# A hybrid attention layer on one core: the head gates as Silu in place, the multiplications one at a time, and the probabilities split ahead of normalising

## The chip, the cores and the metric

The kernel runs on one core of one Trainium2 chip. The metric is the device time of one execution in microseconds (us). Before the change three runs gave 320.87, 321.19 and 321.32 us, a median of 321.19.

## What is computed

One decoder layer on x of 512 tokens by 1024 columns, all in float32. After an RMSNorm a single projection gives eight pieces; attention runs over two groups of eight heads of 64 columns; each group's output is multiplied by the silu of a projected gate; then come an output projection, a residual, a gated second projection and a last norm.

```python
proj = rms_norm(x, norm_g) @ w_in            # a_q a_k a_v a_g b_q b_k b_v b_g
a_out = swa_attention(a_q, a_k, a_v, sinks, bias)    # window of 128, 2 key/value heads
b_out = moba_attention(b_q, b_k, b_v, bias)          # here all past blocks plus the own one
mixed = concat([a_out * silu(a_g), b_out * silu(b_g)])
x = x + mixed @ w_out
gate = sigmoid(rms_norm(x, ple_g) @ w_ple_gate)
return rms_norm(x + (p @ w_ple_proj) * gate, final_norm)
```

## The kernel before

Every float32 operand of TensorE is split into a high part (ScalarE copies it to the format fp32r) and a low part (VectorE subtracts the copy), and each product is three matmuls: high by high, high by low, low by high. `split_T` (lines 141 to 144) does this for activations and probabilities, `Weights.split` (lines 103 to 119) for a quarter of a weight chunk. With `engines="AP"` every second low quarter is subtracted on GpSimd instead of VectorE (line 117); only the two chunks `w_bg` of the second gate are made so (line 163).

There are three phases. The first prepares the norm, the transposed activations `acts` and the small projection. The second, which the change touches, runs the remaining projections as a stream of 192 pieces and lays the attention between them. A piece is three matmuls of 512 columns, or six of 256. `block` (line 424) strings pieces together and runs the evacuation of one accumulator behind the first piece of the next block. Accumulators of the projections share two PSUM slots (tag `acc`), so a block can begin only when the block before the last has been evacuated. The order of blocks is gates and queries of the window heads (`w_qg`), then `w_bv[0]`, `w_bkq[0]`, `w_bkq[1]`, `w_bv[1]`, `w_bkq[2]`, `w_bkq[3]` and the two `w_bg`. Weights are loaded and split by `prefetch` during the sixteen pieces before they are needed.

`swa_step` (line 714) does one of 16 steps of the window heads: scores, bias and maximum (VectorE, line 554), exponential (ScalarE, 557), division, transposition, split, two selects on GpSimd (582), and the product with the values. `moba_step` (line 758) does the same for the second group, 32 steps of one head and one query block, and six to drain. In a step, scores for head h are started, a share of the stream runs, the row sums are divided out (`norm`; for the widest block on ScalarE, line 619, else on VectorE, 621), the transposed probabilities of head h-1 are split into `pt` (`moba_trans`, `split_T`), more of the stream runs, and the product of an earlier group is made by `moba_av` (line 636) from its `pt`.

The gates are evacuated raw into tiles G (`raw_g`, line 524): seven by ScalarE, the eighth by VectorE (529). `silu_gate` (532) then takes a scratch tile of the tag `aux` (two buffers, shared with the evacuations of the attention outputs), computes the sigmoid on ScalarE (534), multiplies it by G on VectorE (535), and multiplies the head outputs O by that on GpSimd (536). It is called for gates 0 to 3 behind the window steps (line 749), for 4 and 5 after the drain step m = 33, for 6 and 7 at the end, where O is split into `acts` (line 799). The tiles G are four slots, so gate 4 takes the place of gate 0.

The order of TensorE and of the transfers queued on SP is the order in which the program is written (`MANUAL`, line 34). From `early.close()` (706) to the last phase's second half (922) the order of ScalarE, VectorE and GpSimd is chosen when the program is built, by the order of the text and by which operations are ready; each engine then works through its queue in that order, and the first operation that has to wait holds up all behind it.

The third phase (from 802) has the output projection (`w_late[0]`, from line 876, four accumulators of which two are the `acc` slots), the second projection and the final norm. Its sigmoids (line 899) come late.

Of the kernel before, what the change touches and what calls it, by code (L numbers as in the profile page):

```python
# [10 lines left out]
F32 = mybir.dt.float32  # L11
BF16 = mybir.dt.bfloat16
F32R = mybir.dt.float32r
AF = mybir.ActivationFunctionType
ALU = mybir.AluOpType

P = 128
SEQ = 512
# [16 lines left out]
C_AQ, C_AK, C_AG, C_BQ, C_BK, C_BV, C_BG = 0, 512, 768, 1280, 1792, 2304, 2816  # L35
# [3 lines left out]
def hybrid_layer_kernel(  # L39
# [16 lines left out]
    nc = tc.nc  # L56
# [22 lines left out]
    def bank(shape, name, tag):  # L79
        return psum.tile(shape, F32, name=name, tag=tag)  # L80
# [75 lines left out]
    def chunk(name, cols, **kw):  # L156
        return Weights(name, [wi[:, :, c:c + n] for c, n in cols], **kw)
# [2 lines left out]
    w_qg = [chunk(f"aqg{c}", [(C_AQ + c * P, P), (C_AG + c * P, P)]) for c in range(4)]  # L160
    w_bv = [chunk(f"bv{n}", [(C_BV + n * 256, 256)]) for n in range(2)]
    w_bkq = [chunk(f"bkq{n}", [(C_BK + n * P, P), (C_BQ + n * P, P)]) for n in range(4)]
    w_bg = [chunk(f"bg{n}", [(C_BG + n * 256, 256)], engines="AP") for n in range(2)]

    def wide(src, n, name, pool=None):
        ns = slice(n * 512, (n + 1) * 512)
# [219 lines left out]
    with ExitStack() as ph2:  # L386
        def pool(name, bufs):
            return ph2.enter_context(tc.tile_pool(name=name, bufs=bufs, reuse_waits="tile"))
# [8 lines left out]
        xa = pool("xa", 2)  # L397

        O = [op.tile([P, SEQ], F32, name=f"O_{c}") for c in range(8)]
        G = {}  # L400
# [3 lines left out]
        def toep(head, swa):  # L404

            if swa:
                b = bp.tile([P, 2, 256], F32, name="b_a", tag="b")
                src = bass.AP(tensor=d_tab.tensor, offset=d_tab.offset + head * JT + JB,
                              ap=[[1, P], [JT, 2], [1, 256]])
            else:  # L410
                b = bp.tile([P, 512], F32, name="b_b", tag="b")
                src = bass.AP(tensor=d_tab.tensor, offset=d_tab.offset + (HA + head) * JT,
                              ap=[[1, P], [1, 512]])
            nc.sync.dma_start(b, src)
            return b
# [16 lines left out]
        def run(n):  # L432
            while stream and (n > 0 or stream[0][0] == 0):
                c, f = stream.popleft()
                n -= c
                f()
# [87 lines left out]
        def raw_g(c, acc):  # L524
            g = op.tile([P, SEQ], F32, name=f"G_{c}", tag=f"G_{c % 4}")
            if c < 7:
                nc.scalar.activation(g, acc, AF.Copy)
            else:
                nc.vector.tensor_copy(g, acc)  # L529
            G[c] = g  # L530

        def silu_gate(c):
            sg = xa.tile([P, SEQ], F32, name="sg", tag="aux")
            nc.scalar.activation(sg, G[c], AF.Sigmoid)
            nc.vector.tensor_mul(sg, sg, G[c])  # L535
            nc.gpsimd.tensor_mul(O[c], O[c], sg)  # L536


        def swa_scores(c, i, q, kt, bias):
            lo_k = 0 if i else P  # L540
            w = 256 - lo_k
            k0 = (i - 1) * P + lo_k
            S = bank([P, 2, 256], "S", "S")
            st = sp.tile([P, 2, 260], F32, name="st", tag="st")
            nm = small.tile([P, 2], F32, name="nm")
            sm = small.tile([P, 2], F32, name="sm")
            ri = small.tile([P, 2], F32, name="ri")
            nc.gpsimd.tensor_copy(st[:, :, 256], nsink[:, 2 * c:2 * c + 2])
            for s in range(2):
                for j in range(2):  # L550
                    nc.tensor.matmul(S[:, s, lo_k:], q[s][:, i, :], kt[:, j, k0:k0 + w],
                                     start=j == 0, stop=j == 1)
            for s in range(2):
                nc.vector.tensor_tensor_reduce(st[:, s, lo_k:256], S[:, s, lo_k:], bias[:, s, lo_k:], -1.0,  # L554
                                               nsink[:, 2 * c + s:2 * c + s + 1], ALU.add, ALU.min,
                                               nm[:, s:s + 1])
                nc.scalar.activation(st[:, s, lo_k:257], st[:, s, lo_k:257], AF.Exp,  # L557
                                     bias=nm[:, s:s + 1], scale=-1.0, accum_out=sm[:, s:s + 1])

            def norm():  # L560
                pv = st[:, :, P:2 * P]
                if i:
                    nc.gpsimd.tensor_add(pv, pv, st[:, :, 0:P])
                nc.vector.reciprocal(ri, sm)
                for s in range(2):
                    nc.vector.tensor_scalar_mul(pv[:, s], pv[:, s], ri[:, s:s + 1])
            return st, norm
# [35 lines left out]
        def moba_scores(h, i, q, kt, bias):  # L603
            w = (i + 1) * P
            S = bank([P, 512], "Sb", "S")
            st = sp.tile([P, 520], F32, name="stb", tag="st")
            nm = small.tile([P, 1], F32, name="nmb")
            sm = small.tile([P, 1], F32, name="smb")
            ri = small.tile([P, 1], F32, name="rib")
            for j in range(2):  # L610
                nc.tensor.matmul(S[:, :w], q[:, i, :], kt[:, j, :w], start=j == 0, stop=j == 1)  # L611
            nc.vector.tensor_tensor_reduce(st[:, :w], S[:, :w], bias[:, 512 - w:], -1.0, 1.0e38,  # L612
                                           ALU.add, ALU.min, nm)
            nc.scalar.activation(st[:, :w], st[:, :w], AF.Exp, bias=nm, scale=-1.0, accum_out=sm)  # L614

            def norm():
                nc.vector.reciprocal(ri, sm)
                if i == 3:
                    nc.scalar.activation(st[:, :w], st[:, :w], AF.Copy, scale=ri)
                else:  # L620
                    nc.vector.tensor_scalar_mul(st[:, :w], st[:, :w], ri)
            return st, norm
# [3 lines left out]
        def moba_trans(g, sts):  # L626
            tp = bank([P, 512], "tpb", "tp")
            o = 0
            for j in GRP[g]:
                for i in range(j, NT):  # L630
                    nc.tensor.transpose(tp[:, o:o + P], sts[i][:, tok(j)], rev)  # L631
                    o += P
            pt = pp.tile([P, 2, 512], F32R, name="pt", tag="pt")
            return lambda: split_T(pt[:, 0, :o], pt[:, 1, :o], tp[:, :o]), pt

        def moba_av(h, g, pt, oacc):
            o = 0
            for j in GRP[g]:
                w = SEQ - j * P
                for l in range(2):  # L640
                    nc.tensor.matmul(oacc[:, j * P:], Vb[:, j, h].rearrange("p a d -> p (a d)"),  # L641
                                     pt[:, l, o:o + w], start=j == 0 and l == 0, stop=j == 3 and l == 1)
                o += w
# [20 lines left out]
        for c in range(4):  # L664
            w = w_qg[c]
            proj_T(w, 0, lambda acc, c=c: make_q(qa[c], acc))
            proj_T(w, P, lambda acc, c=c: raw_g(c, acc))
            ahead(w)
# [78 lines left out]
        swa_step(16)  # L747
        swa_step(16)
        for c in range(4):
            silu_gate(c)  # L750
        run(12)


# [4 lines left out]
        def moba_step(m):  # L758
            h, i = divmod(m, 4)
            norm = None  # L760
            if h < HB:
                if i == 0 and h + 2 < HB:
                    bb[h + 2] = toep(h + 2, False)
                st, norm = moba_scores(h, i, qb[h // 2][h % 2], kb[h // 2][h % 2], bb[h])
                sts[h, i] = st
            pace(per * 0.4)
            if norm:
                norm()
            new = None
            if h > 0 and i > 0 and h - 1 < HB:  # L770
                sp_, pt = moba_trans(i - 1, [sts[h - 1, k] for k in range(NT)])
                sp_()
                new = (h - 1, i - 1, pt)
            pace(per * 0.4)
            if ptq:
                h2, g2, pt2 = ptq.popleft()
                if g2 == 0:
                    ob[h2] = bank([P, 512], "oaccb", "o")
                moba_av(h2, g2, pt2, ob[h2])
                if g2 == 2:  # L780
                    moba_evac(h2, ob[h2])
            if new:
                ptq.append(new)
            pace(per * 0.2)

        for m in range(32):
            moba_step(m)
        per = 2.0
        for m in range(32, 38):
            moba_step(m)  # L790
            if m == 33:
                for c in (4, 5):
                    silu_gate(c)
        run_all()
# [7 lines left out]
    with ExitStack() as ph3:  # L802
# [82 lines left out]
        for t in range(NT):  # L885
            acc = bank([P, 512], "acc4", tags.popleft())
# [36 lines left out]
        for n in range(2):  # L923
            for t in range(NT):
                last = n == 1 and t == NT - 1
                parts = [slice(0, 512)] if not last else [slice(0, 256), slice(256, 512)]
                for cols in parts:
                    w = cols.stop - cols.start
                    acc = bank([P, 512], "acc5", tags.popleft())
# [61 lines left out]
```

## Time and profile before

| | before |
|---|---|
| three runs | 320.87, 321.32, 321.19 us |
| profiled execution | 321.41 us, span 319.7 us, outside the span 1.7 us |
| busy, share of the span | TensorE (PE) 96%, VectorE (DVE) 71%, ScalarE (ACT) 58%, GpSimd (POOL) 21% |
| granted TensorE clock | 0.995 of full speed |
| window heads | about 44 to 125 us |
| second group of heads | about 134 to 221 us |
| output projection onward | from 219.6 us |

All stretches are in microseconds from the start of the span. TensorE's busy time counts a matmul until its modelled end, so matmuls overlap in it and a short wait can hide inside a busy stretch. In a timeline row the first number is the start, the second the duration; a bracket at the end says how long the engine had stood idle before it and whose end released it.

### The profile page before, as it was taken

The numbers are of one execution on the slowest core, as the hardware profiler recorded it, in microseconds if no ns is written. First come the engines' busy times: TensorE is split into PE (matmuls) and PEld (weight loads), VectorE is DVE, ScalarE is ACT, GpSimd is POOL, SyncE is SP. The second block draws the span as 40 slices with busy tenths as digits, with TensorE's granted clock in tenths as the row PEclk, the third lists the DMA queues.
The fourth block names the chain that finished last, engine by engine and source line by source line (L and its number), as shares of the span: only waits on it lengthen the run. The fifth ranks groups of instructions, "written<-read, shape, count | busy, mean of one in ns | idle before, by whom it ended". The sixth has DMA issues, their size and how long they took to land.

```text
span 319.7 us, 4741 instructions
## 1 busy us (share of the span) xinstructions
PE 307.7 (96%) x1651; PEld 259.8 (81%) x1651; DVE 226.3 (71%) x517; ACT 185.6 (58%) x418; POOL 66.6 (21%) x118
## 2 busy tenths in 40 slices
PE   8999999999999999899999999999999999999990
PEld 6788788888889888699888878877888888888890
DVE  2885867886787858878778787859658656672544
ACT  3766565756574638778678776787158323541341
POOL 1420102436343252600003130012300110000011
PEclk9999999999999999999999999999999999999998
DMA  7964597050406083751445303004956700000113
GB/s 237 388 166 114 152 230 232 6 133 1 131 3 199 1 196 87 178 163 37 131 98 143 90 3 131 0 0 111 381 184 248 262 2 0 2 0 0 68 67 131
DMA packets 33208, 37.61 MB, mean 118 GB/s; under 512 B 1416, under 2 KB 24976, under 8 KB 33184
## 3 DMA queue, kind: packets, MB, share of 16 engines
q1 hardware_dynamic: 32240, 34.47, 34.7%
q0 software_dynamic: 800, 2.62, 4.1%
q8 instruction: 13, 0.21, 0.3%
q10 hardware_dynamic: 144, 0.21, 0.2%
q14 instruction: 11, 0.09, 0.1%
HBM read 32.52 MB, written 2.16 MB: 108 GB/s over the span
## 4 chain that ended last, share of the span: by engine, by line
PE 73%; DVE 12%; issue 6%; ACT 4%; POOL 3%; POOLq 0%; DVEq 0%; ACTq 0%
PE acc L451 8%; PE acc L452 8%; PE acc L453 8%; PE acc L137 7%; PE acc L139 7%; PE acc L138 7%; PE acc_ple L282 4%; PE acc_akv L301 4%; PE Sb L611 3%; PE accv L137 2%; PE oaccb L641 2%; PE accv L139 2%; PE accv L138 2%; PE tpb L631 2%; DVE q L499 2%
## 5 line engine op out<-in xcount | busy, mean ns | idle before, releaser
L557 ACT ACTIVATE st<-st,nm 128x257 f32<-128x257 f32 (+1 forms) x32 | 15.2, 478 | 22.0 <-DVE nm L554 19.9
L137 PE MATMUL acc<-hi_wg,h 128*128 128x512 f32 (+1 forms) x72 | 26.7, 370 | 0.0
L139 PE MATMUL acc<-hi_wg,h 128*128 128x512 f32 (+1 forms) x72 | 26.4, 367 | 0.0
L451 PE MATMUL acc<-acts,hi_bkq 128*128 128x512 f32 x64 | 26.4, 412 | 0.0
L138 PE MATMUL acc<-lo_wg,h 128*128 128x512 f32 (+1 forms) x72 | 26.3, 365 | 0.0
L451 PE MATMUL acc<-acts,hi_aqg 128*128 128x512 f32 x64 | 26.2, 410 | 0.0
L137 PE MATMUL acc<-hi_wo,acts 128*128 128x512 f32 x64 | 25.4, 397 | 0.5 <-DVE G L529 0.5
L453 PE MATMUL acc<-acts,lo_aqg 128*128 128x512 f32 x64 | 25.2, 393 | 0.0
L453 PE MATMUL acc<-acts,lo_bkq 128*128 128x512 f32 x64 | 25.1, 392 | 0.0
L138 PE MATMUL acc<-lo_wo,acts 128*128 128x512 f32 x64 | 25.1, 392 | 0.0
L139 PE MATMUL acc<-hi_wo,acts 128*128 128x512 f32 x64 | 25.1, 392 | 0.0
L452 PE MATMUL acc<-acts,hi_bkq 128*128 128x512 f32 x64 | 25.1, 392 | 0.0
L452 PE MATMUL acc<-acts,hi_aqg 128*128 128x512 f32 x64 | 25.1, 392 | 0.0
L614 ACT ACTIVATE stb<-stb,nmb 128x128 f32<-128x128 f32 (+3 forms) x32 | 17.9, 558 | 9.0 <-DVE nmb L612 8.7
L582 POOL TENSOR_SCALAR_AFFINE_SELECT pta<-pta 128x512 fp32r<-128x512 f32 x24 | 17.3, 722 | 14.3 <-DVE pta L144 13.2
L137 PE MATMUL accv<-hi_bv,acts 128*128 128x256 f32 x64 | 18.7, 293 | 1.5 <-DVE kt L144 1.5
L536 POOL TENSOR_TENSOR O<-O,sg 128x512 f32<-128x512 f32 x8 | 11.4, 1430 | 39.4 <-DVE sg L535 39.3
L139 PE MATMUL accv<-hi_bv,acts 128*128 128x256 f32 x64 | 18.1, 282 | 0.0
L138 PE MATMUL accv<-lo_bv,acts 128*128 128x256 f32 x64 | 18.0, 281 | 0.0
L839 ACT ACTIVATE sq<-x 128x512 f32<-128x512 f32 x15 | 9.5, 630 | 13.9 <-DVE x L901 11.6
L612 DVE CUSTOM_DVE_ANT_0 stb<-Sb,b_b 128x128 f32<-128x128 f32 (+3 forms) x32 | 15.5, 485 | 2.4 <-PE Sb L611 2.3
L508 POOL DMA_DIRECT2D kt<-kt x10 | 5.6, 564 | 50.7 <-DVE kt L144 48.3
(165 smaller groups left out, 873.2 us busy)
## 6 DMA issues: line engine op xcount, KB each, us to landing
raw_aqg<-in_w_in_dram SPq DMA_DIRECT2D x8, 512.0 KB, 5.7
raw_bkq<-in_w_in_dram SPq DMA_DIRECT2D x8, 512.0 KB, 5.1
raw_wo<-in_w_out_dram SPq DMA_DIRECT2D x4, 1024.0 KB, 6.5
raw_wg<-in_w_ple_gate_dram SPq DMA_DIRECT2D x4, 1024.0 KB, 5.9
kt<-kt POOLq DMA_DIRECT2D x10, 256.0 KB, 4.5
x_t<-in_x_dram SPq DMA_DIRECT2D x4, 512.0 KB, 7.3
raw_bv<-in_w_in_dram SPq DMA_DIRECT2D x2, 1024.0 KB, 5.4
b_b<-d_tab SPq DMA_DIRECT2D x8, 256.0 KB, 5.8
```

Source lines behind the costliest of these rows:

```text
L137: nc.tensor.matmul(acc, sh, mh, start=first, stop=False)
L138: nc.tensor.matmul(acc, sh, ml, start=False, stop=False)
L139: nc.tensor.matmul(acc, sl, mh, start=False, stop=last)
L282: nc.tensor.matmul(pacc[t, n], (pTl if j == 1 else pTh)[:, k, tok(t)], (wpl if j == 2 else wph)[:, n, k], start=k == 0 and j == 0, stop=k ...
L301: nc.tensor.matmul(akv[m], w_[:, k, cs], acts[:, k, a_, :], start=k == 0 and w_ is w_akv.hi and a_ == 0, stop=k == KC - 1 and w_ is w_akv.lo)
L451: nc.tensor.matmul(acc, w.hi[:, k, cs], acts[:, k, 0, :], start=k == 0, stop=False)
L452: nc.tensor.matmul(acc, w.hi[:, k, cs], acts[:, k, 1, :], start=False, stop=False)
L453: nc.tensor.matmul(acc, w.lo[:, k, cs], acts[:, k, 0, :], start=False, stop=k == KC - 1)
L557: nc.scalar.activation(st[:, s, lo_k:257], st[:, s, lo_k:257], AF.Exp, bias=nm[:, s:s + 1], scale=-1.0, accum_out=sm[:, s:s + 1])
L582: nc.gpsimd.affine_select(out=pt[:, :, b, :].rearrange("p j (s q) -> p j s q", s=2), in_=pt[:, :, 1, :].rearrange("p j (s q) -> p j s q", ...
L612: nc.vector.tensor_tensor_reduce(st[:, :w], S[:, :w], bias[:, 512 - w:], -1.0, 1.0e38, ALU.add, ALU.min, nm)
L614: nc.scalar.activation(st[:, :w], st[:, :w], AF.Exp, bias=nm, scale=-1.0, accum_out=sm)
```

## The change

There are five edits. The low halves of `w_bg` are all made on VectorE. The eighth gate leaves PSUM as Silu on ScalarE, and not as a copy on VectorE. The other seven are turned into their silu in place by one ScalarE operation each (`silu`), which replaces the sigmoid, its scratch tile and the product on VectorE; each is issued behind the last exponential traced by then (`issue_after` puts it later in the same queue and adds no wait). The product with O is called apart, on GpSimd for gates 0 to 5 (0 to 3 after the steps 1, 4, 7 and 10 of the second group), on VectorE for 6 and 7. In `moba_step` the division `norm` is traced behind the transposition and split.

```diff
-    w_bg = [chunk(f"bg{n}", [(C_BG + n * 256, 256)], engines="AP") for n in range(2)]
+    w_bg = [chunk(f"bg{n}", [(C_BG + n * 256, 256)]) for n in range(2)]
...
             if c < 7:
                 nc.scalar.activation(g, acc, AF.Copy)
             else:
-                nc.vector.tensor_copy(g, acc)
+                with tc.issue_after(last_exp[0].ins):
+                    nc.scalar.activation(g, acc, AF.Silu)
             G[c] = g
 
         def silu_gate(c):
-            sg = xa.tile([P, SEQ], F32, name="sg", tag="aux")
-            nc.scalar.activation(sg, G[c], AF.Sigmoid)
-            nc.vector.tensor_mul(sg, sg, G[c])
-            nc.gpsimd.tensor_mul(O[c], O[c], sg)
+            (nc.vector if c >= 6 else nc.gpsimd).tensor_mul(O[c], O[c], G[c])
+
+        def silu(c):
+
+            with tc.issue_after(last_exp[0].ins):
+                nc.scalar.activation(G[c], G[c], AF.Silu)
+
+        last_exp = [None]
...
-                nc.scalar.activation(st[:, s, lo_k:257], st[:, s, lo_k:257], AF.Exp,
+                last_exp[0] = nc.scalar.activation(st[:, s, lo_k:257], st[:, s, lo_k:257], AF.Exp,
...
-            nc.scalar.activation(st[:, :w], st[:, :w], AF.Exp, bias=nm, scale=-1.0, accum_out=sm)
+            last_exp[0] = nc.scalar.activation(st[:, :w], st[:, :w], AF.Exp, bias=nm, scale=-1.0, accum_out=sm)
...
         for c in range(4):
-            silu_gate(c)
+            silu(c)
         run(12)
...
             pace(per * 0.4)
-            if norm:
-                norm()
             new = None
             if h > 0 and i > 0 and h - 1 < HB:
                 sp_, pt = moba_trans(i - 1, [sts[h - 1, k] for k in range(NT)])
                 sp_()
                 new = (h - 1, i - 1, pt)
+            if norm:
+                norm()
             pace(per * 0.4)
...
         for m in range(32):
             moba_step(m)
+            if m in (1, 4, 7, 10):
+                silu_gate((m - 1) // 3)
         per = 2.0
         for m in range(32, 38):
             moba_step(m)
             if m == 33:
+                for c in range(4, 7):
+                    silu(c)
                 for c in (4, 5):
                     silu_gate(c)
```

## Rows read from the trace of the kernel before

**Rows 1.** Windows: length, busy us (count) of PE, PEld, DVE, ACT, POOL; clock, DMA share, GB/s

```profile
128.00:141.00 13.00, 11.48 (x80) 10.39 (x80) 11.79 (x25) 8.99 (x18) 4.70 (x5) 1.00 0.59 151
141.00:162.00 21.00, 21.00 (x133) 18.85 (x133) 15.78 (x50) 15.35 (x38) 1.02 (x2) 1.00 0.42 121
162.00:192.00 30.00, 29.45 (x158) 24.61 (x158) 24.72 (x68) 23.27 (x54) 6.46 (x6) 1.00 0.32 73
...
224.00:312.00 88.00, 88.00 (x424) 73.42 (x423) 52.96 (x80) 35.03 (x75) 9.13 (x24) 1.00 0.31 110
```

**Rows 2.** Waits of the whole run: waiter, releaser, us in total, times, longest

```profile
PE oaccb L641 <- DVE pt L144: 0.6, 2, 0.4
...
PEld oaccb L641 <- DVE pt L144: 2.3, 4, 0.8
...
ACT sg L899 <- PE acc L139: 9.2, 6, 2.6
```

**Rows 3.** Timeline from the last window step to the second group's first scores

```profile
123.45 1.28 ACT L534 ACT_TABLE_LOAD   x1
...
127.89 0.63 ACT L534 ACTIVATE sg<-G 128x512 f32<-128x512 f32 x1 [1.37 <-POOL O L536]
...
128.56 3.02 DVE L535 TENSOR_TENSOR sg<-sg,G 128x512 f32<-128x512 f32 x2 [1.26 <-ACT sg L534]
...
129.80 0.59 ACT L143 ACTIVATE kt<-acc 64x512 fp32r<-64x512 f32 x1
...
131.61 0.69 DVE L144 TENSOR_TENSOR kt<-acc,kt 64x512 fp32r<-64x512 f32 x1
...
132.45 0.36 PE L137 MATMUL accv<-hi_bv,acts 128*128 128x256 f32 x1 [1.52 <-DVE kt L144]
```

**Rows 4.** Timeline of the next evacuation and the block that needs its slot

```profile
135.17 0.69 DVE L499 SCALAR_TENSOR_TENSOR q<-acc,q 64x512 fp32r<-64x512 f32 x1
...
136.01 0.36 PE L137 MATMUL accv<-hi_bv,acts 128*128 128x256 f32 x1
```

**Rows 5.** Groups by line: operation, count, busy us in total, mean ns, idle before

```profile
L118 DVE TENSOR_TENSOR lo_wo<-raw_wo,hi_wo 128x512 fp32r<-128x512 f32 x16 | 10.4, 685 | 6.2 <-ACT hi_wo L116 6.1
...
L118 DVE TENSOR_TENSOR lo_bg<-raw_bg,hi_bg 128x512 fp32r<-128x512 f32 x4 | 3.7, 922 | 0.4 <-ACT hi_bg L116 0.4
...
L118 POOL TENSOR_TENSOR lo_bg<-raw_bg,hi_bg 128x512 fp32r<-128x512 f32 x4 | 5.3, 1334 | 16.1 <-ACT hi_bg L116 16.1
...
L536 POOL TENSOR_TENSOR O<-O,sg 128x512 f32<-128x512 f32 x8 | 11.4, 1430 | 39.4 <-DVE sg L535 39.3
```

**Rows 6.** Timeline of GpSimd and VectorE ahead of a late split

```profile
185.17 1.30 POOL L118 TENSOR_TENSOR lo_bg<-raw_bg,hi_bg 128x512 fp32r<-128x512 f32 x1 [6.11 <-ACT hi_bg L116]
...
185.52 1.50 DVE L118 TENSOR_TENSOR lo_bg<-raw_bg,hi_bg 128x512 fp32r<-128x512 f32 x1
...
187.85 0.42 DVE L621 TENSOR_SCALAR stb<-stb,rib 128x384 f32<-128x384 f32 x1
188.30 0.56 DVE L144 TENSOR_TENSOR pt<-tpb,pt 128x384 fp32r<-128x384 f32 x1
```

**Rows 7.** Waits from 212 to 225 us

```profile
PEld oaccb L641 <- DVE pt L144: 1.1, 2, 0.5
```

**Rows 8.** Timeline from the last normalisation to the output projection

```profile
209.03 0.72 ACT L619 ACTIVATE stb<-stb,rib 128x512 f32<-128x512 f32 x1 [0.32 <-DVE rib L617]
...
210.79 0.60 PE L631 MATMUL tpb<-rev,stb 128*128 128x128 f32 x4
...
210.86 1.28 ACT L534 ACT_TABLE_LOAD   x1
...
214.45 0.97 DVE L535 TENSOR_TENSOR sg<-sg,G 128x512 f32<-128x512 f32 x1 [0.31 <-ACT sg L534]
...
221.57 0.69 DVE L529 COPY G<-acc 128x512 f32<-128x512 f32 x1
...
222.32 0.50 PE L137 MATMUL acc<-hi_wo,acts 128*128 128x512 f32 x1 [0.47 <-DVE G L529]
```

## The prediction

> **What bounds the kernel now.** I read the windows first, for the share of each engine in each stretch. TensorE's own work is the bound almost everywhere: from 224 us on it is busy for 88.00 of 88 us, and from 141 to 162 us for all 21.00 [rows 1]. No saving on another engine is worth anything there. What can be won is the time in which TensorE stands still, so I then listed its waits, and looked up each in the timeline. In the part that the change touches there are three.
>
> The largest, 1.52 us, is at 132.45: the first matmul of the values' projection wants an accumulator slot, and that slot is still being evacuated (kt, VectorE, 131.61) [rows 3]. Two queues made this late. On ScalarE the third sigmoid stands 1.37 us waiting for GpSimd to free its scratch tile, and the second half of the key's evacuation is queued behind the sigmoids and starts at 129.80. On VectorE two gate products take 3.02 us, 1.51 each, and kt follows them at once.
>
> The second is the product with the values, which waits for the split probabilities pt. TensorE's matmuls show 0.6 us idle in two places, its weight loads 2.3 us in four [rows 2]; two of the four, 1.1 us, fall between 212 and 225 us [rows 7], so 1.2 us fall before. The third, 0.47 us, is at 222.32, where the output projection wants the slot of the eighth gate, which VectorE copies only at 221.57 [rows 8].
>
> **The gates behind the window heads.** The change takes away four scratch tiles, four VectorE products and ScalarE's wait for GpSimd. ScalarE's work stays: four Silus instead of four sigmoids, taken at the sigmoid's 0.63 us, and the load of a table before them, 1.28 us [rows 3]. The key's second half could then start no later than 127.89, where the waiting sigmoid stood. VectorE's part would end near 128.5 + 0.69 = 129.2, and TensorE wants the slot at 132.45 - 1.52 = 130.93. So the whole 1.52 us goes.
>
> What is late next is the evacuation of the query block: it ends at 135.17 + 0.69 = 135.86, and the block that needs its slot starts at 136.01 [rows 4], so there was no slack. If TensorE comes 1.52 us earlier, the evacuation must too. It can give back between nothing (the 3.02 us of products and the late kt are gone from ahead of it) and all 1.52. I take 0.3, nearer to nothing, since its queue gains about twice what it must.
>
> **The low quarters.** Four subtractions of 1.334 us leave GpSimd and become four of 0.685 us on VectorE: 2.74 us more. The four that VectorE had already took 922 ns instead of 685 beside GpSimd [rows 5], so 4 x 0.237 = 0.95 us comes back, 1.8 us net, between 162 and 192 us where VectorE is busy for 24.72 of 30 us [rows 1]. The price on the path lies between nothing and 1.8. I take nothing: from 141 to 162 us VectorE makes all the quarters of another chunk, and TensorE has no gap there [rows 1].
>
> **Splitting ahead of dividing.** In rows 6 the late pt at 188.30 stands behind a quarter that GpSimd stretched to 1.50 us (0.82 too long) and behind a division of 0.42 us. Both go from ahead of it, another quarter comes. The division is needed a step later at the earliest, by the transpositions of the next head. Of the 1.2 us before 212 I count half, 0.6.
>
> Between 212 and 225 us VectorE loses the products of gates 4 and 5, one of 0.97 us at 214.45 [rows 8], from ahead of pt; all 1.1 us should go. Together 1.7, between the 0.6 of the matmuls' idle time and the 2.3 of the weight loads.
>
> **The eighth gate.** ScalarE evacuates it as Silu, some 0.6 us after its block. The slot is wanted at 222.32 - 0.47 = 221.85, two us after the block's end. So 0.47 us goes; it stays if ScalarE's queue has weight copies ahead of it.
>
> **The silus behind the last exponential.** This is new and costs something. Behind that exponential ScalarE idles 0.32 us until the reciprocal for its division at 209.03 is there [rows 8]. Gate 4 is ready long before, so its Silu can be queued into that gap, with its table load: free at 208.71, plus 1.28, plus 0.63, the division starts at 210.62 and ends at 211.34. The transpositions that need it run at 210.79, so TensorE would lose 0.55. With two silus in the gap it is 1.18, with none nothing. I take 0.5. Before, the load stood at 210.86, behind the division.
>
> **The products on GpSimd.** Four of 1.430 us [rows 5] move from about 126 to 133 us into the steps of the second group, unless the queue takes them as soon as they are ready. GpSimd has 1.02 us of work there [rows 1]. VectorE pays: a two-input operation beside GpSimd went from 0.685 to 1.50 us [rows 5, 6], so up to 4 x 0.82 = 3.3 us, with 21 - 15.78 = 5.2 us idle in that stretch. Their cost is between nothing and 3.3; I take nothing, with VectorE's idle time as cover. Transfers of kt issued from GpSimd's queue may start up to 1.43 us later; their keys are used several steps on.
>
> In rows 6 GpSimd runs from 185.17 to 186.47, and VectorE's subtraction from 185.52 to 187.02. The Trainium skill, page "SBUF — State Buffer", section "Who interferes with whom", says that a VectorE instruction with two SBUF inputs and a GpSimd instruction that reads SBUF exclude each other: the later one waits for the whole of the earlier. By that rule the subtraction would end at 186.47 + 0.685 = 187.16; the trace has 187.02, so it agrees within 0.14 us. By the rule the four products could block VectorE for 5.7 us instead of 3.3, which speaks against the change (an estimate).
>
> **Edits at no cost.** The two products of gates 6 and 7 on VectorE stand where TensorE has 88 us of work without a gap [rows 1]; the gates are needed only after six eighths of the first output block. A further table load before the sigmoids of line 899 (no row shows whether one is needed) costs between nothing and 1.28; ScalarE waits 9.2 us for TensorE in front of them [rows 2], so nothing. No transfer of the SP queue is moved.
>
> **Sum.** 1.52 + 1.7 + 0.47 - 0.3 - 0.5 = 2.89 us. The profiled execution took 321.41, 0.22 over the median of 321.19. Against the median: 318.3 us.
>
> **Rivals.** (A) ScalarE takes the silus as blocks. Behind the window heads 1.28 + 4 x 0.63 = 3.8 us would stand ahead of an evacuation and could rebuild the 1.52 us; at the end two silus cost 1.18 instead of 0.5. That gives 318.3 + 1.5 + 0.7 = 320.5. For it: nothing but readiness keeps them apart. Against: each goes into the queue only where ScalarE has nothing older.
>
> (B) The wait only moves. TensorE, early by 1.52, waits for the query's evacuation for all of it, 1.2 more than I took, and the two late splits before 212 stay: 318.3 + 1.2 + 0.6 = 320.1. For it: rows 4 show no slack. Against: the 3.02 us that leave VectorE.
>
> (C) Slower: VectorE becomes the bound between 141 and 192 us. It gains 1.8 us of quarters and 3.3 us of collisions, and if each step waits for its pt, all 5.1 us reach TensorE, and the 0.6 does not come: 318.3 + 5.1 + 0.6 = 324.0. It decides from the point where pt ends after TensorE wants it in most steps. For it: 24.72 of 30 us, and two late splits there. Against: they are two among some sixteen groups, and 141 to 162 us runs without a wait.
>
> (D) The queues don't do what the text says: the eighth Silu behind the weight copies, the 0.47 stays: 318.8.
>
> **The numbers.** The forecast has 0.60, A 0.13, B 0.12, C 0.09, D 0.06. The range begins at 321.19 - (1.52 + 2.3 + 0.47) = 316.9, with every wait gone and nothing given back, and reaches to 320.4, over B and D and up to A; C is left out. A difference of 0.2%, 0.64 us, is about the least that a measurement of this kernel tells from none, so faster is below 320.55: the forecast, D, and most of A and B, 0.80. Same takes the rest of A and B, 0.09. Slower is C and a little for what I don't see, 0.11.
>
> **What would show it.** Right: no gap of TensorE near 131 us, the key's evacuation done before 130; pt ahead of the division on VectorE; no wait on G at the output projection; from then on the same work, some 3 us earlier. The 0.5 shows as a table load between the last exponential and the division of line 619. Wrong: waits of line 641 on pt in many steps (C), a gap at the second values' block (B), four Silus in a row ahead of a key's evacuation (A). If the gap at 131 is gone and the time is still the same, the sum's mistake lies in what is late next.

## The result and the profile after

Four runs of each kernel on one chip: before 321.16 us (320.87 to 321.32), after 317.84 us (317.46 to 318.12). The ratio on record is 0.9891 with an interval of 0.9879 to 0.9904 (the two medians alone give 0.9897): faster by 3.32 us, about 1%. The forecast was 318.3, within 316.9 to 320.4. The profiled execution of after took 317.72 us, 316.0 of them the span and 1.7 outside it, as before.

The page's first part (TensorE's share is up by one point, VectorE's and GpSimd's are down), and behind it the first and the third window of [rows 1]:

```profile
PE 306.3 (97%) x1651; PEld 259.7 (82%) x1651; DVE 218.7 (69%) x514; ACT 186.5 (59%) x419; POOL 58.1 (18%) x112
```

```profile
128.00:141.00 13.00, 12.58 (x93) 11.89 (x92) 8.41 (x26) 8.78 (x20) 0.51 (x1) 1.00 0.73 194
...
162.00:192.00 30.00, 30.00 (x163) 25.48 (x162) 26.59 (x73) 23.75 (x55) 1.12 (x2) 1.00 0.30 77
```

From 128 to 141 us TensorE is busy for 12.58 us instead of 11.48. From 162 to 192 us TensorE has no gap any more. VectorE has 26.59 us of work there instead of 24.72, but the two windows do not hold the same work, since after is about 2 us ahead. The groups by line compare like with like: the low quarters `lo_bg` take VectorE 5.4 us instead of 3.7 [rows 5], near the 1.8 more that the prediction worked out.

The waits of the whole run on these places, answering [rows 2]:

```profile
PE accv L137 <- DVE q L499: 0.4, 1, 0.4
...
PE oaccb L646 <- DVE pt L144: 0.2, 1, 0.2
...
PEld oaccb L646 <- DVE pt L144: 0.5, 1, 0.5
```

The waits on `pt` fell from 0.6 to 0.2 (matmuls) and from 2.3 to 0.5 (weight loads). A wait on `q` is new.

**Where the time came from.** Both traces hold the same 1651 matmuls in the same order, so the start of the n-th matmul can be set against its start before. The shift between them changes in a few places only (0.1 us and more; the next matmul's share of 0.1 is counted in):

| start of the matmul, before and after | what it had waited for | change, us |
|---|---|---|
| 132.45, 130.44 first values' block | evacuation of the key, `kt` | -1.68 |
| 136.01, 134.34 second values' block | evacuation of the query, `q` | +0.41 |
| 171.11, 169.14 product with the values | `pt` | -0.31 |
| 188.91, 186.43 product with the values | `pt` | -0.67 |
| 211.12, 208.67 last transpositions | division of line 624 | +0.14 |
| 214.19, 211.48 product with the values | `pt` | -0.42 |
| 222.32, 218.79 output projection | eighth gate | -0.75 |

That is -3.28 us. Ahead of them the shift changes by some 0.3 us in the first 20 us, at the first transfers and the warm-up, which the change does not touch and which differ from one execution to another (by up to 1 us in the runs below). So I count from matmul 121 (line 267, at about 23 us) to the end: 296.46 us before, 293.12 after, 3.34 less. In this count small effects can be read that the medians can't tell apart.

The first place, answering [rows 3], in after's timeline:

```profile
111.60 0.18 ACT L562 ACTIVATION_READ_ACCUMULATOR st<-st,nm 128x1 f32 x1
111.80 1.28 ACT L539 ACT_TABLE_LOAD   x1
113.10 0.63 ACT L539 ACTIVATE G<-G 128x512 f32<-128x512 f32 x1
...
113.81 1.28 POOL L534 TENSOR_TENSOR O<-O,G 128x512 f32<-128x512 f32 x1 [0.94 <-ACT G L539]
...
115.14 1.14 ACT L539 ACTIVATE G<-G 128x512 f32<-128x512 f32 x2
...
126.54 0.59 ACT L143 ACTIVATE kt<-acc 64x512 fp32r<-64x512 f32 x1 [0.75 <-DVE kt L144]
...
127.17 0.69 DVE L144 TENSOR_TENSOR kt<-acc,kt 64x512 fp32r<-64x512 f32 x1 [0.66 <-ACT kt L143]
...
130.21 0.39 PE L453 MATMUL acc<-acts,lo_bkq 128*128 128x512 f32 x1
130.44 0.28 PE L137 MATMUL accv<-hi_bv,acts 128*128 128x256 f32 x1
...
133.50 0.69 DVE L499 SCALAR_TENSOR_TENSOR q<-acc,q 64x512 fp32r<-64x512 f32 x1
134.34 0.36 PE L137 MATMUL accv<-hi_bv,acts 128*128 128x256 f32 x1 [0.42 <-DVE q L499]
```

The first four Silus stand right behind the last exponential of the window heads, at 111 to 118 us, among evacuations. The key's second half starts at 126.54 instead of 129.80, `kt` ends at 127.86, and the matmul of 130.44 has no wait. The query's evacuation comes 1.67 us earlier (133.50, before 135.17), TensorE 2.01: hence the new wait of 0.42. The four products on GpSimd did not go into the second group's steps; its queue took them from 113.81 on, the last at 125.20.

The end of the second group, answering [rows 7, 8], in the same timeline:

```profile
205.24 0.73 ACT L619 ACTIVATE stb<-stb,nmb 128x512 f32<-128x512 f32 x1
206.08 1.28 ACT L539 ACT_TABLE_LOAD   x1
207.37 0.63 ACT L539 ACTIVATE G<-G 128x512 f32<-128x512 f32 x1
207.91 0.71 ACT L624 ACTIVATE stb<-stb,rib 128x512 f32<-128x512 f32 x1
...
210.94 1.31 POOL L534 TENSOR_TENSOR O<-O,G 128x512 f32<-128x512 f32 x1 [1.58 <-ACT G L539]
...
211.42 1.38 DVE L534 TENSOR_TENSOR O<-O,G 128x512 f32<-128x512 f32 x1 [0.34 <-ACT G L539]
212.72 0.55 DVE L144 TENSOR_TENSOR pt<-tpb,pt 128x384 fp32r<-128x384 f32 x1
213.19 1.88 DVE L144 TENSOR_TENSOR acts<-O,acts 128x512 fp32r<-128x512 f32 x3
214.99 0.55 DVE L144 TENSOR_TENSOR pt<-tpb,pt 128x384 fp32r<-128x384 f32 x1
...
215.59 0.56 PE L646 MATMUL oaccb<-pt,Vb 128*128 128x256 f32 x3 [0.17 <-DVE pt L144]
...
217.35 0.60 ACT L530 ACTIVATE G<-acc 128x512 f32<-128x512 f32 x1
...
218.79 0.39 PE L137 MATMUL acc<-hi_wo,acts 128*128 128x512 f32 x1
```

One load and one Silu stand ahead of the last division, as the prediction had them. The eighth gate leaves at 217.35, and the output projection runs on. The product of gate 6 on VectorE took 1.38 us instead of 0.69, beside GpSimd's product at 210.94. It stands ahead of the `pt` of 212.72, for which TensorE does not wait. The wait that is left, at 215.59, is for the next `pt` (214.99), and what stands directly ahead of that one are three subtractions for `acts`. A further load before the sigmoids of line 908, at 271.82, is needed (five loads, before four); it runs in their wait.

### The profile page after: what moved, and what is told of

Its sections match the earlier page's. It is cut to its first block, busy times and chain, and to the rows that moved or that the text cites. A ratio compares the mean times of both kernels' runs of the same rounds, so it can differ in the third digit from the quotient of the medians.

```text
span 316.0 us, 4739 instructions
## 1 busy us (share of the span) xinstructions
PE 306.3 (97%) x1651; PEld 259.7 (82%) x1651; DVE 218.7 (69%) x514; ACT 186.5 (59%) x419; POOL 58.1 (18%) x112
## 4 chain that ended last, share of the span: by engine, by line
PE 77%; DVE 8%; issue 5%; ACT 5%; POOL 3%; POOLq 0%; ACTq 0%; DVEq 0%
PE acc L451 9%; PE acc L452 9%; PE acc L453 8%; PE acc L139 8%; PE acc L137 8%; PE acc L138 8%; PE acc_ple L282 4%; PE acc_akv L301 4%; PE Sb L616 3%; PE oaccb L646 3%; PE tpb L636 2%; PE accv L137 2%; PE accv L139 2%; PE accv L138 2%; ACT st L562 1%
## 5 line engine op out<-in xcount | busy, mean ns | idle before, releaser
L118 DVE TENSOR_TENSOR lo_wo<-raw_wo,hi_wo 128x512 fp32r<-128x512 f32 x16 | 10.3, 685 | 9.3 <-ACT hi_wo L116 9.1
```

## The experiments

My theory: the gain is the sum of separate waits of TensorE, each taken away by its own edit, and VectorE's load is not the bound (against rival C). The rivals for the largest term: it is the place of the gates' work in the queues, or it is the work taken from VectorE.

### The edits one at a time

Four kernels are before with one edit each. `b_silu` has the in-place silus, issued early, with everything else of before (its eighth gate is copied by VectorE and made Silu at the end):

```diff
-            sg = xa.tile([P, SEQ], F32, name="sg", tag="aux")
-            nc.scalar.activation(sg, G[c], AF.Sigmoid)
-            nc.vector.tensor_mul(sg, sg, G[c])
-            nc.gpsimd.tensor_mul(O[c], O[c], sg)
+            (nc.vector if c >= 6 else nc.gpsimd).tensor_mul(O[c], O[c], G[c])
...
+        def silu(c):
...
+            with tc.issue_after(last_exp[0].ins):
+                nc.scalar.activation(G[c], G[c], AF.Silu)
...
```

> The kernel before with the Silu scheme alone: gates turned into Silu in place behind the last exponential, products called apart, the eighth gate still copied by VectorE; low quarters on GpSimd and the division ahead of the split as before. My theory: the gap of 1.52 us of idle at the first values' block goes (1.7 us of TensorE's time), about 0.4 comes back at the second values' block, the two waits on pt behind 212 us shrink by about 0.5, the gap in front of the last transpositions costs 0.1 to 0.5; the waits near 171 and 189 us and the 0.6 us at the output projection stay. About 319.5 us, ratio 0.993 to 0.997. Rival: the gap is VectorE's general lateness, and without the other edits half of it stays: above 320.3 us.

`b_g7` lets ScalarE copy the eighth gate:

```diff
-                nc.vector.tensor_copy(g, acc)
+                nc.scalar.activation(g, acc, AF.Copy)
```

> The kernel before with the eighth gate alone evacuated by ScalarE (a copy) instead of VectorE. My theory: the wait of the output projection goes, 0.5 to 0.64 us, and nothing else changes: 320.6 us, ratio 0.998. Rival: the copy falls behind the weight copies in ScalarE's queue, or the slot is late for another reason: 321.2 us, the wait stays.

`b_norm` traces `norm()` behind `moba_trans` and `sp_()`, and `b_low` takes `engines="AP"` from `w_bg`, each as in the change's diff.

> The kernel before with the split traced ahead of the division alone. My theory: the wait at 189 us (a division of 0.42 us ahead of pt) loses about 0.5 us; the one at 171 us, which has only a reciprocal ahead of it, stays: 320.7 us, ratio 0.998 to 0.9995. Rival: the low quarters on GpSimd make both waits, and the order alone changes nothing: 321.2 us.

> The kernel before with the low quarters of the second gate's weights all on VectorE, nothing else. My theory: VectorE gains four subtractions of 0.685 us and loses 0.95 us of collisions; the wait at 189 us gets no shorter, or by up to 0.3 us, the one at 171 us may grow: 321.2 us, ratio 0.999 to 1.002. Rival: the collision of 0.82 us is what makes pt late at 189 us, and taking it away alone ends that wait: 320.5 us.

Before ran at 321.17 us beside them. The last column is the time from matmul 121 to the end, less that of before:

| kernel | median, us | ratio to before (interval) | trace, us |
|---|---|---|---|
| b_silu | 319.49 | 0.9951 (0.9939 to 0.9964) | -1.61 |
| b_g7 | 320.62 | 0.9980 (0.9971 to 0.9989) | -0.83 |
| b_norm | 320.86 | 0.9987 (0.9979 to 0.9996) | -0.46 |
| b_low | 320.93 | 0.9994 (0.9984 to 1.0003) | -0.23 |

All four ratios lie where I had given them. The four traces add up to -3.13 of the -3.34 us: for the most part the edits act on separate waits. Each shows in its own rows of the table of shifts. `b_silu` has -1.68 and +0.42 at the two values' blocks, +0.19 at the last transpositions and -0.42 at the product of 214. `b_g7` has -0.75 at the output projection. Its timeline has the copy where after has its Silu:

```profile
220.45 0.60 ACT L529 ACTIVATE G<-acc 128x512 f32<-128x512 f32 x1
```

`b_norm` and `b_low` share two places: -0.20 and -0.13 at 171 us, where I had expected nothing of `b_norm`, -0.46 and -0.21 at 189. Together these are -0.33 and -0.67, near the -0.31 and -0.67 of the whole change; `b_norm` gives 0.22 back two products later. Its timeline, against [rows 6]:

```profile
185.28 1.49 DVE L118 TENSOR_TENSOR lo_bg<-raw_bg,hi_bg 128x512 fp32r<-128x512 f32 x1
...
187.60 0.56 DVE L144 TENSOR_TENSOR pt<-tpb,pt 128x384 fp32r<-128x384 f32 x1
188.08 1.13 DVE L621 TENSOR_SCALAR stb<-stb,rib 128x384 f32<-128x384 f32 x1
```

`pt` starts 0.70 us earlier than the 188.30 of before (0.24 us of that was won ahead of it), with the stretched quarter still ahead of it. Now it is the division that GpSimd stretches, to 1.13 us from 0.42: GpSimd's next quarter runs from 187.70 to 188.99. `b_low` alone is too small for its times to tell it from nothing.

### Place or work

`b_early` keeps the sigmoid, VectorE's product and GpSimd's product, and only moves them: issued behind the last exponential, with a scratch tile from the ring of `st`, so that none waits for the tag `aux`.

```diff
-            sg = xa.tile([P, SEQ], F32, name="sg", tag="aux")
-            nc.scalar.activation(sg, G[c], AF.Sigmoid)
+            sg = sp.tile([P, 520], F32, name="sg", tag="st")[:, 0:SEQ]
+            with tc.issue_after(last_exp[0].ins):
+                nc.scalar.activation(sg, G[c], AF.Sigmoid)
...
```

> The kernel before with sigmoid and both products kept, but the sigmoid is issued behind the last exponential and its scratch is taken from the larger ring of probability tiles instead of the two tiles shared with the evacuations. My theory: the gap at 131 us comes from where the gate work stands (late, behind scratch tiles), not from VectorE's share in it; placed at 112 to 120 us, where VectorE has idle time, the same four products cost nothing: gap gone (1.68 us), 0.4 us back at the second values' block, up to 0.5 us back in front of the last transpositions. About 320.0 us, ratio 0.994 to 0.998. Rival: the product on VectorE is the cause; moved, it delays another evacuation, and TensorE's total does not shorten: 321.2 us or more.

320.47 us beside a before of 321.51, ratio 0.9961 (0.9945 to 0.9977). The first values' block gains the whole 1.68 us with VectorE's four products still there, so it was their place and the scratch tile that made the gap. But the work isn't free at its new place. TensorE loses 0.80 us that neither before nor after loses:

```profile
114.88 1.30 POOL L537 TENSOR_TENSOR O<-O,sg 128x512 f32<-128x512 f32 x1 [1.67 <-DVE sg L536]
116.13 1.68 POOL L585 TENSOR_SCALAR_AFFINE_SELECT pta<-pta 128x512 fp32r<-128x512 f32 x2
...
117.86 0.51 PE L594 MATMUL oacc<-pta,Va 128*128 128x256 f32 x2 [0.54 <-POOL pta L585]
```

GpSimd's product came later, behind VectorE's, and held up its selects, for which the product with the values waits. With Silu in place the first product came at 113.81 and this wait is absent. `b_early` also gains 0.61 us at the output projection, without the edit of the eighth gate: VectorE's copy of that gate starts at 220.48, before at 221.57. So that wait, too, depends on what stands ahead in VectorE's queue, and the edit is one way to end it.

### Why the silus are tied to an exponential

`a_free` is the changed kernel without the two `issue_after`:

```diff
...
-            with tc.issue_after(last_exp[0].ins):
-                nc.scalar.activation(G[c], G[c], AF.Silu)
+            nc.scalar.activation(G[c], G[c], AF.Silu)
```

> The changed kernel with the Silus not held behind an exponential: each stands in ScalarE's queue where it is ready first, which is between exponentials, so each pair costs a load of the Silu table and one back, 2.56 us of ScalarE. My theory: four such pairs in the window steps, where the probabilities' chain already runs through ScalarE, VectorE and GpSimd, put 2 to 6 us on TensorE: 320 to 324 us. Rival: the loads fall into ScalarE's idle time and cost nothing: 317.8 us, and the order behind the last exponential is worth nothing.

324.46 us beside a before of 321.54, ratio 1.0098 (1.0085 to 1.0111): slower than before, and 0.46 us over the upper end of what I had given. Its groups by line have 13 loads of tables for the Silus and the exponentials, and two elsewhere; after has five in all.

```profile
L537 ACT ACT_TABLE_LOAD x7 | 9.0, 1283 | 0.1
...
L560 ACT ACT_TABLE_LOAD x4 | 5.1, 1283 | 0.1
...
L617 ACT ACT_TABLE_LOAD x2 | 2.6, 1283 | 0.0
```

A Silu whose gate is ready stands between two exponentials, and there are ten loads more. Six of them are followed by a load back for an exponential, four times in the window heads and twice in the second group. TensorE loses time behind four of these six pairs. Behind the third, VectorE stands idle for 0.98 us until the exponential is done, and TensorE waits for the division that follows:

```profile
81.02 1.28 ACT L537 ACT_TABLE_LOAD   x1
82.31 0.63 ACT L537 ACTIVATE G<-G 128x512 f32<-128x512 f32 x1
82.96 1.28 ACT L560 ACT_TABLE_LOAD   x1
...
86.34 0.30 PE L577 MATMUL tp<-rev,st 128*128 128x128 f32 x1 [1.65 <-DVE st L569]
```

TensorE stands still for 1.65 us in front of this transposition. From matmul 121 to the end `a_free` loses 6.55 us against after, more than the 3.34 us that the whole change won. Without the tie the change would have been a loss.

### What the changed kernel still loses

`a_gap` ties the silus of gates 4 to 6 to the last division instead of the last exponential, to take back the load ahead of it:

```diff
-                    nc.scalar.activation(st[:, :w], st[:, :w], AF.Copy, scale=ri)
+                    last_exp[0] = nc.scalar.activation(st[:, :w], st[:, :w], AF.Copy, scale=ri)
```

`a_both` is `a_gap`, and also ties the high quarters of `w_bkq[2]` behind the evacuation of the query, so that their subtractions do not stand ahead of `q` on VectorE:

```diff
+            if self.name == "bkq2":
+                with tc.issue_after(last_q[0].ins):
+                    nc.scalar.activation(hi[:, sl], self.raw[:, sl], AF.Copy)
...
-                nc.scalar.activation(q[a], ar[a], AF.Copy, scale=SCALE)
+                last_q[0] = nc.scalar.activation(q[a], ar[a], AF.Copy, scale=SCALE)
```

> The changed kernel with the Silus of gates 4 to 6 issued behind the last division instead of the last exponential. My theory: the 0.14 to 0.19 us in front of the last transpositions come back, unless the table load then delays the next split: between 317.5 and 318.0 us, not to be told from the changed kernel. Rival: the gap of ScalarE is the best place for the load, and behind the division it makes a wait on pt of up to 0.6 us: 318.4 us.

> As the previous one, and the high quarters of the third key and query chunk are issued behind the last part of the query's evacuation in front of them. My theory: the wait at the second values' block (0.41 us) shrinks by 0.3, since the evacuation no longer waits behind weight quarters on either engine: about 317.4 us, ratio 0.986 to 0.990. Rival: the two halves of the evacuation take as long alone, because each half reads the same slot in turn; the wait stays, and the weight quarters, later by 2 us, delay the first exponentials: 317.9 us or more.

317.47 and 317.45 us beside a before of 321.51, both 0.9867 (0.9844 to 0.9891 and 0.9843 to 0.9891). Neither can be told from the changed kernel's 0.9891 by its times. By the traces `a_gap` is 0.22 us shorter than after from matmul 121 on, 0.14 of it at the last transpositions, and `a_both` 0.36. In `a_both` the wait of 0.42 on `q` is gone, 0.58 us at its place, but 0.53 comes back at a product with the values:

```profile
147.22 1.89 DVE L124 TENSOR_TENSOR lo_bkq<-raw_bkq,hi_bkq 128x512 fp32r<-128x512 f32 x3
...
149.70 0.56 PE L652 MATMUL oaccb<-pt,Vb 128*128 128x256 f32 x3 [0.21 <-DVE pt L150]
```

The quarters that were put off came three in a row ahead of a `pt`. That is rival B at small scale: the wait moved.

`a_tail` goes on from `a_gap` and gives GpSimd gate 6's product too (`c >= 7` in place of `c >= 6`). In `a_gap` this product (211.88, 1.37 us) stands ahead of a `pt` for which TensorE waits at 213.78. In after it does not: there the wait is one product with the values later, as shown above, and the expectation that follows has this wrong.

> The changed kernel with the Silus of gates 4 to 6 behind the last division, and the product of gate 6 on GpSimd instead of VectorE. In the changed kernel that product takes 1.38 us on VectorE, beside GpSimd's product, ahead of a split that TensorE waits for. My theory: that wait (0.2 to 0.5 us) goes: about 317.2 us, ratio 0.985 to 0.989. Rival: the subtractions for the output projection move up into the place and make the next split as late: 317.5 us.

318.31 us beside a before of 321.54, ratio 0.9907 (0.9895 to 0.9920): my expectation fell. The wait at 213.78 is gone, but what the rival describes came, and cost more than its 317.5 us: from matmul 121 on `a_tail` is 0.56 us longer than after. Three subtractions of line 144 for `acts` stand ahead of the next `pt`, beside two products on GpSimd, and take 2.93 us, where `a_gap` has two in 1.28:

```profile
213.45 2.93 DVE L144 TENSOR_TENSOR acts<-O,acts 128x512 fp32r<-128x512 f32 x3
...
216.90 0.56 PE L646 MATMUL oaccb<-pt,Vb 128*128 128x256 f32 x3 [0.99 <-DVE pt L144]
```

### Is VectorE near the bound?

`a_coll` puts into the second group's steps what rival C had feared: ten sums on GpSimd, each reading SBUF for about the time of a product. They write into the tile of `G[0]` after its use.

```diff
+            if 2 <= m < 16 and m % 4 < 3:
+                b_ = bb[m // 4 + 2]
+                nc.gpsimd.tensor_add(G[0], b_, b_)
```

> The changed kernel with ten more operations on GpSimd between about 137 and 170 us, each a sum of a bias tile with itself written into a gate slot that is free by then (two inputs from SBUF, 128x512, about 1.3 us; the output is not used). My theory: each stretches at most one VectorE operation by up to 0.8 us, VectorE's idle time takes most of it, and TensorE loses 0 to 1.0 us: 317.8 to 318.8 us. Rival C of the prediction: VectorE has no slack in these steps, and ten collisions of 0.8 us reach TensorE as 5 to 8 us: above 322 us.

319.54 us beside a before of 321.51, ratio 0.9930 (0.9907 to 0.9953). I had expected at most 318.8, rival C over 322. From matmul 121 on it is 1.45 us longer than after. The timeline at the largest loss, +0.90 at the third values' block:

```profile
134.32 3.93 POOL L797 TENSOR_TENSOR G<-b_b 128x512 f32<-128x512 f32 x3 [0.97 <-DMA b_b<-d_tab]
...
134.86 1.04 DVE L118 TENSOR_TENSOR lo_bkq<-raw_bkq,hi_bkq 128x512 fp32r<-128x512 f32 x1
...
137.47 0.87 DVE L626 TENSOR_SCALAR stb<-stb,rib 128x128 f32<-128x128 f32 x1
...
139.62 0.35 PE L137 MATMUL accv<-hi_bv,acts 128*128 128x256 f32 x1 [0.74 <-DVE Vb L144]
```

And the groups by line of its divisions (first fence) against those of after (second):

```profile
L626 DVE TENSOR_SCALAR stb<-stb,rib 128x128 f32<-128x128 f32 x8 | 3.1, 384 | 0.3
```

```profile
L626 DVE TENSOR_SCALAR stb<-stb,rib 128x128 f32<-128x128 f32 x8 | 2.3, 287 | 0.3
```

GpSimd stretches not only the subtractions, 0.69 to 1.04 us, but also the divisions, which have one tensor as input: 287 to 384 ns on average. The one at 137.47 took 0.87 us beside GpSimd, one of the same shape at 142.74 without it 0.29. In the same trace the operations with one operand in PSUM keep their times: `pt` with 512 columns took 0.68 us beside a sum, at 145.64 and at 154.81, and 0.69 at 164.51 without one. The Trainium skill, page "SBUF — State Buffer", section "Who interferes with whom", names `tensor_scalar` with copies and casts among the operations that can take both of VectorE's ports and then exclude GpSimd; this trace agrees with that. So VectorE is not the bound in these steps, but it has little to spare: the ten sums reach TensorE with 1.45 us, 0.15 each on average. Four such products there would have cost some 0.6 us (an estimate from that), had the queue not taken them earlier.

### The two small edits, undone

`a_ap` is after with `engines="AP"` for `w_bg` again, `a_order` is after with `norm()` ahead of `moba_trans` again.

> The changed kernel with every second low quarter of the second gate back on GpSimd. My theory: the four quarters are a small part; the waits on pt that the low quarters alone shortened by 0.13 and 0.21 us come back in part: 317.9 to 318.3 us, 0.1 to 0.4 us over the changed kernel. Rival: with the split ahead of the division there is slack for the collision, and nothing changes: 317.8 us.

> The changed kernel with the division back ahead of the transposition and split. My theory: the two waits on pt come back less what the low quarters took, 0.2 and 0.35 us: 318.2 to 318.6 us. Rival: without GpSimd's quarters VectorE has slack enough, and the order changes nothing: 317.8 us.

318.78 us, ratio 0.9914 (0.9902 to 0.9925), and 318.72 us, 0.9918 (0.9905 to 0.9931), beside a before of 321.54. Both medians lie above what I had given, but before, too, ran 0.38 us slower beside them than beside after (321.54, not 321.16), and by their intervals the ratios can hardly be told from after's 0.9891. The traces say more: from matmul 121 on the two lose 0.53 and 0.60 us against after, at the products with the values of 169 to 188 us, where I had given 0.1 to 0.4 and 0.4 to 0.8. Taken out of after, each costs more than it brought alone (0.23 and 0.46); where the other is there it is worth somewhat more.

## Why the prediction was right

The time came out 0.46 us under the forecast; the sum was 2.89 us, the medians moved by 3.32 and the traces by 3.34. The steps, in its order:

- **The gap at 131.** Predicted 1.52 gone and 0.3 given back at the query's evacuation; measured 1.68 and 0.41. That there was no slack in [rows 4] was right, and 0.41 lies near the end that I chose. `b_early` shows the cause: the place of the gates' work with its scratch tiles, not VectorE's share of it.
- **Low quarters and order, before 212 us.** Predicted 0 for the quarters and 0.6 for the order; measured 0.98 together, 0.31 at 171 and 0.67 at 189. `b_norm` has 0.46 of it and `b_low` 0.23 alone. Taking the quarters at nothing was too cautious: the collisions they end were ahead of the late `pt` of [rows 6].
- **The waits on `pt` after 212 us.** This term was mis-sized: "all 1.1 us should go", measured 0.42 at the product of 214, and less than 0.1 at the one of 218. The step that failed is that VectorE loses the products of gates 4 and 5 "from ahead of pt". The one of 0.97 us at 214.45 stands ahead of the `pt` of 215.34, for which TensorE did not wait. Ahead of the `pt` of the second wait stood subtractions for `acts`, already before:

```profile
215.81 2.13 DVE L144 TENSOR_TENSOR acts<-O,acts 128x512 fp32r<-128x512 f32 x2
217.87 0.55 DVE L144 TENSOR_TENSOR pt<-tpb,pt 128x384 fp32r<-128x384 f32 x1
...
218.47 0.56 PE L641 MATMUL oaccb<-pt,Vb 128*128 128x256 f32 x3 [0.20 <-DVE pt L144]
```

They stand there in after too (213.19), and so this wait stayed, 0.5 us of the weight load. At 214 ScalarE's load of 210.86 [rows 8] left as well as VectorE's product; which of the two the 0.42 us is owed to is not shown. And a weight load waits while the matmul before it still runs, so not all of its wait is lost: at 214 it waited 0.54 us.

- **The eighth gate.** Predicted 0.47; measured 0.75, here and in `b_g7`. The bracket counts only the time in which no matmul ran. In an unbroken stream a matmul starts while the one before still runs (above, the one of 130.21 is 0.39 us long and the next starts 0.23 later), and those 0.16 us are lost too: 0.47 + 0.16 = 0.63, close to the 0.64 of the waiting matmul, and the one behind it lost another 0.11. The gap at 131 agrees: 1.52 + 0.16 = 1.68.
- **The Silu ahead of the last division.** Predicted as a load and one Silu there and 0.5 us; the rows are as predicted, the loss is 0.14. The step that failed is "the transpositions that need it run at 210.79": only the fourth of those four reads the row block of the last division (`moba_trans`, k = 3), 0.33 us later. By the same sum, 211.34 - 211.12 = 0.22.
- **The products on GpSimd, and the load at the end.** Both cost nothing, as taken. The products because the queue took them when they were ready, which the prediction had left open; the load of line 908 in ScalarE's wait.

The total was right to 0.46 us because the misses of 0.6 (waits on `pt` after 212) on one side and of 0.38 (before 212), 0.28 (eighth gate) and 0.36 (Silu) on the other partly cancelled. That they did is luck: the single terms were less good than their sum.

Of the rivals, A's pair of Silus appeared at 115.14 without a cost, since no evacuation was late there. Of B only the wait on `q` came, 0.41 us of the 1.5 that it feared. C did not come, and `a_coll` shows that even ten sums on GpSimd, for the four products, do not bring it. D is excluded by the row at 217.35. No version I ran can be told from the changed kernel as faster; by the trace alone `a_both` is 0.36 us ahead.

## What to carry to other kernels

When an engine's work is taken away, first ask which queue it stood in and what stood behind it: here the same products, moved some ten microseconds earlier, gave the same gain at that place. An activation that needs another table is placed by hand where no exponential follows; left to readiness it cost more than the whole change had won. Count a matmul's wait as the least that is lost and a weight load's only in part, and expect the place of a removed operation to be taken by the next one in the queue, as `a_both` and `a_tail` show.

## What was not expected of the hardware

GpSimd stretches VectorE's division too, a one-input multiplication of SBUF by a column of numbers: from 0.42 to 1.13 us (`b_norm`).

In `a_free` the wait of 1.65 us cost more than itself. The windows from 84 us on (columns as in [rows 1]):

```profile
84.00:86.00 2.00, 0.69 (x3) 0.21 (x2) 0.77 (x5) 1.96 (x9) 0.00 (x0) 1.00 0.41 109
86.00:88.00 2.00, 1.36 (x4) 1.08 (x5) 1.94 (x7) 1.09 (x4) 1.47 (x3) 0.69 1.17 323
88.00:90.00 2.00, 2.00 (x7) 1.57 (x6) 1.32 (x4) 0.89 (x3) 0.73 (x1) 0.50 0.39 92
90.00:92.00 2.00, 2.00 (x13) 1.83 (x13) 1.18 (x4) 0.59 (x1) 0.00 (x0) 0.95 0.00 0
```

TensorE was busy for 0.69 us from 84 to 86 and for 1.36 from 86 to 88. The granted clock fell, to 0.69 on average from 86 to 88 and to 0.50, the level of 1.2 GHz, from 88 to 90; from 90 to 92 it was back near 2.4 GHz, at 0.95. Matmuls that follow each other by 0.23 us in after did so by 0.43 us here: over the matmuls from 83.3 to 84.5 us of after, another 1.3 us was lost that no wait shows.
